# A bias tile that is loaded and masked half a unit ahead of its use, in a hybrid attention step

## The chip, the cores and the metric

One NeuronCore of a Trainium2 chip runs the whole step as one launch. The metric is the device time of a run in microseconds (us), from start to end of the program on the device; of several runs the median counts.

## The reference

One layer of a streaming encoder for 2048 prompt frames of width 1024 (and 32 sample frames, a small side job). `h = RMSNorm(x)`; one projection `z = h @ w_in` gives queries, keys, values and gates for two branches:

- A: chunk-band attention with 8 heads of 64. Frames come in chunks of 64; a frame sees its own chunk and the 8 before it, and its scores get a learned bias of the head, indexed by clipped distance: `scores = q·k / 8 + rel_bias[h, clip(i - j)]`, then softmax and `@ v`.
- B: differential attention, 4 heads with two q/k pairs of 64 and a value of 128. Two softmaxes over all earlier chunks, `p1 - lam * p2`, `@ v`, and an RMSNorm per head. No bias.

Both results are multiplied by `silu(gate)`, joined, projected by `w_out`, added to `x` and normed. New keys and values are outputs too.

## The kernel before, in words

**Units.** The work is cut into eight units, one for each weight slice of 512 columns: four A units (two heads each, u = 0 to 3) and four B units (one head each, u = 4 to 7). Line 701 sets the order: `[0, 4, 5, 1, 6, 2, 7, 3]`, so A, B, B, A, B, A, B, A. Each unit runs over 8 chunks of 256 frames (c = 0 to 7); `steps` (line 711) lists the 64 pairs (n, c) of unit number and chunk.

**A step** (loop of line 734). `chunk_qkv` projects the chunk (matmuls of lines 296 to 298 for keys and values, 303 to 305 for the transposed queries and the gate), every fp32 operand split in a high and a low part, and transposes keys and queries. `get_hT` loads the normed input of the next chunk (lines 261, 288, 289; two buffers). `attn_b` or `attn_a` computes scores (425, 426) and softmax. The second half of the attention (transposes 434, splits 438 and 439, the products with the values 450, and `finish_o` with lines 457 to 461, which stores the chunk's output with the DMA of line 461) is traced one step later, at the end of the step of the next chunk. So step c ends with the store of chunk c - 1.

**The bias.** In an A unit each score block goes through line 577 on VectorE (DVE), which adds a slice of the tile `bias` to the scores in PSUM, writes `ea` and takes the row maximum. `bias` is 128 x 2 x 640 in fp32 (640 KB, one buffer), loaded by one DMA of SyncE's queue (line 743, issued through the helper of line 146), and two corners of it are filled with -1e30 on GpSimd (POOL; lines 744 and 745), which masks what the band does not reach. Load and fills stand at c == 0 of the A unit, ahead of its `chunk_qkv`.

**What sets the order.** The program is traced in Python order, and a list scheduler puts each engine's instructions in one static order: by a priority (position in the trace, moved by `ahead(...)`) among what its own clock holds ready. At run time each engine works its list in order. `dma_here` (line 145) pins its DMA behind the DMA that was traced just before it on SyncE's queue. For the bias of unit n that is the store of line 461 of chunk 6 of unit n - 1, the last DMA traced in step (n - 1, 7). Three score tiles (`s_ps`), two transpose tiles (`t_ps`), one output tile (`o_ps`) and two projection tiles (`z_ps`) share PSUM.

The scheduler runs ahead across units: with the units at 345 to 570 us (n = 2, B) and then n = 3 (A), the projection of the A unit's chunk 0 is done while the B unit's last chunks are still in their attention.

Of the kernel before, what the change touches and what calls it, by code (L numbers as in the profile page):

```python
# [8 lines left out]
F32 = mybir.dt.float32  # L9
# [5 lines left out]
P = 128  # L15
# [9 lines left out]
NEG = -1.0e30  # L25
BAND = 640
# [4 lines left out]
def hybrid_step(  # L31
# [31 lines left out]
    PE, DVE, ACT, POOL, SP = nc.tensor, nc.vector, nc.scalar, nc.gpsimd, nc.sync  # L63
# [19 lines left out]
    pool = ctx.enter_context(tc.tile_pool(name="work", bufs=2))  # L83
# [61 lines left out]
    def dma_here(**kw):  # L145
        tc.keep_in_program_order(SP.dma_start(**kw))

    def small_loads():
        dma_here(out=ropec, in_=rope_c)
        dma_here(out=ropes, in_=rope_s)  # L150
        dma_here(out=gcol, in_=subln)
        DVE.tensor_scalar(gcol, gcol, 1.0 - LAMBDA_INIT, 0.0, ALU.mult, ALU.add)
        lt = e_tile("lt")
        lv = lt[:, 0:256].rearrange("p (a e) -> p a e", a=4)
        dma_here(out=lt[:, 0:256], in_=lams.broadcast_to([P, 256]))
        lp = lt[:, 256:384].rearrange("p (a e) -> p a e", a=2)
        DVE.tensor_tensor(lp, lv[:, 0:4:2, :], lv[:, 1:4:2, :], ALU.mult)
        ls = st_tile("ls", 2, 1)
        DVE.tensor_reduce(ls, lp, AX.X, ALU.add)
        le = st_tile("le", 2, 1)  # L160
        ACT.activation(le, ls, AF.Exp)
        DVE.scalar_tensor_tensor(nlam, le[:, 1:2], LAMBDA_INIT, le[:, 0:1], ALU.subtract, ALU.subtract)
        ACT.copy(out=lamc[NS:2 * NS], in_=nlam[NS:2 * NS])
# [6 lines left out]
    def load_w(wsrc, cur_b, gain=None, tags=(("w", 10),) * KT, raws=None):  # L170
        his, los = [], []
        for k in range(KT):
            raw = raw_w(wsrc, k, cur_b) if raws is None else raws[k]
            tag, bufs = tags[k]
            w = pool.tile([P, 2, 512], F32R, name="w", tag=tag, bufs=bufs)
            hi, lo = w[:, 0, :], w[:, 1, :]
            g = 1.0 if gain is None else gain[:, k:k + 1]
            if raws is not None:
                ACT.activation(hi, raw, AF.Copy, scale=g)  # L179
                DVE.scalar_tensor_tensor(lo, raw, g, hi.bitcast(F32), ALU.mult, ALU.subtract)  # L180
            elif cur_b and gain is not None and k % 2 == 0:
                ACT.activation(hi, raw, AF.Copy, scale=g)
                POOL.tensor_scalar(raw, raw, g, 0.0, ALU.mult, ALU.add)
                POOL.tensor_tensor(lo, raw, hi.bitcast(F32), ALU.subtract)
            else:
                POOL.tensor_scalar(hi, raw, g, 0.0, ALU.mult, ALU.add)
                DVE.scalar_tensor_tensor(lo, raw, g, hi.bitcast(F32), ALU.mult, ALU.subtract)
            his.append(hi)
            los.append(lo)
        return his, los  # L190
# [37 lines left out]
    def load_xT(c, js=range(4)):  # L228
        xs = [e_tile("xT").rearrange("p (k t) -> p k t", k=2) for _ in js]
        for x, j in zip(xs, js):  # L230
            SP.dma_start(out=x, in_=x_t[c, :, 2 * j:2 * j + 2, :])
        return xs

    def load_rows(c):
        return [load_x(x_pv[t * P:(t + 1) * P, :], P) for t in (2 * c, 2 * c + 1)]
# [40 lines left out]
    def make_hTs():  # L276
        h = norm_rows(load_x(x_sv, NS), NS)
        tp = t_psum()
        for k in range(KT):
            j = k % 4  # L280
            PE.transpose(out=tp[:, k * NS:(k + 1) * NS], in_=h[k // 4][0:NS, j * P:(j + 1) * P], identity=ident[0:NS, 0:NS])
        tv = tp[:, 0:KT * NS].rearrange("p (k t) -> p k t", k=KT)
        ACT.copy(out=hTs[:, :, 0:NS], in_=tv)
        DVE.tensor_tensor(hTs[:, :, NS:2 * NS], tv, hTs[:, :, 0:NS].bitcast(F32), ALU.subtract)
# [416 lines left out]
    order = [0, 4, 5, 1, 6, 2, 7, 3]  # L701
# [3 lines left out]
    def finish(gen, late):  # L705
        try:
            gen.send(late)
        except StopIteration:
            pass
# [10 lines left out]
    def get_hT(i):  # L720
        if i >= len(steps):
            return None
        n, c = steps[i]
        if n == 0:
            hT = make_hT(c, xts.pop(c))
            return hT
        return load_T(hT_d[c]), load_scales(c)
# [6 lines left out]
    for i, (n, c) in enumerate(steps):  # L734
        u = order[n]
        isB = u >= 4
        W = Ws[n]
        if c == 0:
            kss, vts = [], []
            bias = None  # L740
            if not isB:
                bias = pool.tile([P, 2, BAND], F32, name="bias", tag="bias", bufs=1)
                dma_here(out=bias, in_=bias_p[:, 2 * u:2 * u + 2, :])
                POOL.memset(bias[0:64, :, BAND - 64:BAND], NEG)
                POOL.memset(bias[64:128, :, 0:64], NEG)
        qkv = chunk_qkv(u, isB, c, hTn, W, kss, vts)
        QH, QL = next(qkv)
        gate = None
        if n == 0 and c + 2 < NCH:
            xts[c + 2] = load_xT(c + 2), load_rows(c + 2)  # L750
        hTn = get_hT(i + 1)
        if n == 0 and c == 1:
            small_loads()
        if n == 1 and c == 1:
            dma_here(out=aksv[0:PAST - NS, :], in_=cakv[NS:PAST, :])
            dma_here(out=avsv[0:PAST - NS, :], in_=cavv[NS:PAST, :])
        if n == 0 and c == NCH - 3:
            make_hTs()
        if c == NCH - 1 and n + 1 < len(order):
            v = order[n + 1]  # L760
            Ws[n + 1] = load_w(w_in[v // 4, v % 4], isB, ngain)
        prev = pend
        pend = attn_b(u, c, kss, vts, QH, QL) if isB else attn_a(u, c, kss, vts, QH, QL, bias)
        next(pend)
        late = (next(qkv), vts[c])
        if prev:
            finish(prev, plate)
        plate = late
        mid = n > 0 and not isB
        if c == 0 or (mid and c == 4):  # L770
            for _ in pend_s or ():
                pass
        if c == (2 if mid else NCH - 2):
            pend_s = sample_unit(u, isB, W)
            next(pend_s)
# [99 lines left out]
```

## Time and profile before

| | us |
|---|---|
| median of three runs (1591.02 to 1595.62) | 1593.42 |
| the profiled execution | 1592.68 |
| its span, first to last instruction | 1590.9 |
| TensorE matmul busy / weight load busy | 1537.6 / 1428.2 |
| DVE / ACT / POOL busy | 1097.6 / 1008.8 / 619.9 |

PE is TensorE's matmul row and PEld its weight loads, which overlap the matmuls; DVE is VectorE, ACT ScalarE, POOL GpSimd, SPq SyncE's queue, which issues every DMA here. The span is 1.8 us shorter than the time of the execution. A wait is read as `engine line <- what ended it`; it is idle time of the waiting engine just before that instruction. TensorE's granted clock is 0.990 of full speed over the span.

### The profile page before, as it was taken

What the parts mean: (1) busy time and instruction counts of PE and PEld (TensorE: products, weight loads), DVE (VectorE), ACT (ScalarE), POOL (GpSimd) and SP (SyncE); (2) the same over time, 40 slices, a digit from 0 to 9 for tenths busy, and PEclk for the clock granted to TensorE, in tenths of its full rate; (3) what the DMA queues carried; (4) which work ended last, traced back from release to release, by engine and by line L of the source; (5) the groups of instructions that cost most, each with busy time, mean ns of one, the idle gap of its engine ahead of it and who ended that gap; (6) DMA issues with size and microseconds to landing.
All of it is one profiled execution on the core that took longest, in us unless ns stands there. A gap on an engine that the chain in (4) does not pass through costs nothing.

```text
span 1590.9 us, 30369 instructions
## 1 busy us (share of the span) xinstructions
PE 1537.6 (97%) x10448; PEld 1428.2 (90%) x10448; DVE 1097.6 (69%) x3045; ACT 1008.8 (63%) x2706; POOL 619.9 (39%) x829
## 2 busy tenths in 40 slices
PE   7999999999999999999999999999999999999997
PEld 7999999888998889999998889999988899978885
DVE  5777768886689856577788756677888565853333
ACT  7885667776677766556777766657777665531111
POOL 5564424564346433343345522433445432520000
PEclk9999999999999999999999999999999999999999
DMA  9964454342442233536432233546432244635552
GB/s 368 366 250 156 166 190 140 112 148 85 174 157 92 71 115 111 196 133 231 143 139 80 91 142 127 186 146 230 148 111 101 90 142 151 235 131 181 167 208 69
DMA packets 105659, 249.65 MB, mean 157 GB/s; under 512 B 11192, under 2 KB 60480, under 8 KB 88064
## 3 DMA queue, kind: packets, MB, share of 16 engines
q1 hardware_dynamic: 105504, 247.70, 44.1%
q8 instruction: 83, 1.36, 0.3%
q14 instruction: 72, 0.59, 0.1%
HBM read 194.83 MB, written 53.75 MB: 156 GB/s over the span
## 4 chain that ended last, share of the span: by engine, by line
PE 80%; DVE 9%; ACT 3%; DMA 3%; issue 2%; POOL 2%; SPq 0%; DVEq 0%; ACTq 0%; POOLq 0%
PE z_ps L296 12%; PE z_ps L297 12%; PE z_ps L298 12%; PE o_ps L450 8%; PE t_ps L434 6%; PE s_ps L425 5%; PE z_ps L303 5%; PE s_ps L426 5%; PE z_ps L304 5%; PE z_ps L305 5%; DVE nmx L517 2%; DVE e L530 2%; DMA bias<-in_bias_p_dram 2%; DVE pl L439 1%; PE z_ps L310 1%
## 5 line engine op out<-in xcount | busy, mean ns | idle before, releaser
L296 PE MATMUL z_ps<-w,hT 128*128 128x256 f32 (+2 forms) x1280 | 421.5, 330 | 8.1 <-ACT w L179 6.5
L297 PE MATMUL z_ps<-w,hT 128*128 128x256 f32 (+2 forms) x1280 | 421.8, 330 | 2.0 <-DVE w L180 1.5
L298 PE MATMUL z_ps<-w,hT 128*128 128x256 f32 (+2 forms) x1280 | 420.8, 329 | 0.0
L296 PEld LDWEIGHTS z_ps<-w,hT 128*128 128x128 f32 x1280 | 243.0, 190 | 22.8 <-ACT w L179 6.5
L297 PEld LDWEIGHTS z_ps<-w,hT 128*128 128x128 f32 x1280 | 243.2, 190 | 17.8 <-DVE w L180 2.2
L298 PEld LDWEIGHTS z_ps<-w,hT 128*128 128x128 f32 x1280 | 243.2, 190 | 13.4
L519 ACT ACTIVATE e<-s_ps,nmx 128x512 f32<-128x512 f32 (+3 forms) x320 | 199.4, 624 | 87.5 <-DVE nmx L517 83.5
L439 DVE TENSOR_TENSOR pl<-t_ps,ph 128x512 fp32r<-128x512 f32 (+1 forms) x312 | 191.7, 623 | 66.8 <-ACT ph L438 63.1
L303 PE MATMUL z_ps<-hT,w 128*128 128x256 f32 x768 | 222.2, 289 | 5.6 <-DVE ql L391 5.6
L304 PE MATMUL z_ps<-hT,w 128*128 128x256 f32 x768 | 221.4, 288 | 0.0
L305 PE MATMUL z_ps<-hT,w 128*128 128x256 f32 x768 | 221.4, 288 | 0.0
L438 ACT CAST ph<-t_ps 128x512 fp32r<-128x512 f32 (+1 forms) x312 | 162.3, 535 | 70.6 <-PE t_ps L434 43.3
L425 PE MATMUL s_ps<-ks,qh 128*128 128x512 f32 (+2 forms) x544 | 194.1, 366 | 10.5 <-ACT e L519 8.6
L517 DVE TENSOR_REDUCE nmx<-s_ps 128x1 f32<-128x512 f32 (+3 forms) x320 | 188.8, 601 | 12.7 <-PE s_ps L426 9.4
L450 PE MATMUL o_ps<-ph,vt 128*128 128x256 f32 (+1 forms) x912 | 182.0, 274 | 8.1 <-DVE on L472 4.4
L426 PE MATMUL s_ps<-ks,ql 128*128 128x512 f32 (+2 forms) x544 | 188.1, 357 | 0.8 <-DVE ql L390 0.8
L525 POOL TENSOR_SCALAR e<-e,da 128x512 f32<-128x512 f32 (+3 forms) x160 | 112.6, 717 | 156.0 <-DVE da L495 103.4
L450 PE MATMUL o_ps<-pl,vt 128*128 128x256 f32 (+1 forms) x624 | 169.8, 311 | 0.1
L584 POOL TENSOR_SCALAR ea<-ea,sma 128x640 f32<-128x640 f32 (+4 forms) x128 | 96.8, 759 | 182.5 <-DVE sma L583 118.6
L450 PEld LDWEIGHTS o_ps<-ph,vt 128*128 128x128 f32 x912 | 149.4, 191 | 12.6 <-ACT ph L438 7.7
L303 PEld LDWEIGHTS z_ps<-hT,w 128*128 128x128 f32 x768 | 147.9, 193 | 9.7 <-DVE ql L391 6.7
L304 PEld LDWEIGHTS z_ps<-hT,w 128*128 128x128 f32 x768 | 147.8, 193 | 3.6 <-issue 1.3
(197 smaller groups left out, 3047.1 us busy)
## 6 DMA issues: line engine op xcount, KB each, us to landing
hT<-hTd SPq DMA_DIRECT2D x112, 1024.0 KB, 5.8
wraw<-in_w_in_dram SPq DMA_DIRECT2D x64, 256.0 KB, 4.9
hTd<-hT SPq DMA_DIRECT2D x8, 2048.0 KB, 9.4
oTd<-oT SPq DMA_DIRECT2D x64, 256.0 KB, 5.6
hT<-oTd SPq DMA_DIRECT2D x16, 1024.0 KB, 7.0
out_dram<-z SPq DMA_DIRECT2D x160, 64.0 KB, 1.6
xT<-in_x_t_dram SPq DMA_DIRECT2D x32, 256.0 KB, 5.2
xt<-in_x_prompt_dram SPq DMA_DIRECT2D x32, 256.0 KB, 5.7
```

The source lines that it names most:

```text
L296: PE.matmul(zp, hT[:, 0, k, ts], his[k][:, cols], start=(k == 0), stop=False)
L297: PE.matmul(zp, hT[:, 0, k, ts], los[k][:, cols], start=False, stop=False)
L298: PE.matmul(zp, hT[:, 1, k, ts], his[k][:, cols], start=False, stop=(k == KT - 1))
L303: PE.matmul(zp, his[k][:, cols], hT[:, 0, k, :], start=(k == 0), stop=False)
L304: PE.matmul(zp, his[k][:, cols], hT[:, 1, k, :], start=False, stop=False)
L305: PE.matmul(zp, los[k][:, cols], hT[:, 0, k, :], start=False, stop=(k == KT - 1))
L425: PE.matmul(sp[:, 0:w], QH[:, m, qs], ks[:, m, kc], start=True, stop=False)
L426: PE.matmul(sp[:, 0:w], QL[:, m, qs], ks[:, m, kc], start=False, stop=True)
L439: DVE.tensor_tensor(lv, tv, hv.bitcast(F32), ALU.subtract)
L450: PE.matmul(o, v, p, start=(first and n == 0), stop=(last and n == len(seq) - 1))
L517: DVE.tensor_reduce(nmx[:, m, b:b + 1], sp[:, 0:w], AX.X, ALU.max, negate=True)
L519: ACT.activation(e[:, 0:w], sp[:, 0:w], AF.Exp, bias=nmx[:, m, b:b + 1], accum_out=sm[:, m, b:b + 1])
```

## The change

The `bias` tile is now allocated, loaded and filled at c == 3 of the unit ahead of an A unit (in this order of units that is always a B unit: n = 2, 4 and 6). The first unit has none ahead of it and keeps its load at its own first step. Nothing else is changed: the same DMA, the same two fills, the same single buffer. By the trace order the DMA is now pinned behind the store of chunk 1 of that B unit.

```
         if c == 0:
             kss, vts = [], []
-            bias = None
-            if not isB:
-                bias = pool.tile([P, 2, BAND], F32, name="bias", tag="bias", bufs=1)
-                dma_here(out=bias, in_=bias_p[:, 2 * u:2 * u + 2, :])
-                POOL.memset(bias[0:64, :, BAND - 64:BAND], NEG)
-                POOL.memset(bias[64:128, :, 0:64], NEG)
+        nu = order[n + 1] if n + 1 < len(order) else 4
+        if (c == 3 and nu < 4) or i == 0:
+            lu = u if i == 0 else nu
+            bias = pool.tile([P, 2, BAND], F32, name="bias", tag="bias", bufs=1)
+            dma_here(out=bias, in_=bias_p[:, 2 * lu:2 * lu + 2, :])
+            POOL.memset(bias[0:64, :, BAND - 64:BAND], NEG)
+            POOL.memset(bias[64:128, :, 0:64], NEG)
         qkv = chunk_qkv(u, isB, c, hTn, W, kss, vts)
```

## Rows read from the trace of the kernel before

**Rows 1.** The page, part 1: busy time, share of the span and number of instructions of each engine.
```profile
PE 1537.6 (97%) x10448; PEld 1428.2 (90%) x10448; DVE 1097.6 (69%) x3045; ACT 1008.8 (63%) x2706; POOL 619.9 (39%) x829
```

**Rows 2.** The chain of waits that ended last, in order of time (start us, us, what): its longest pieces but for the first 15 us.
```profile
570.21 8.18 DMA bias<-in_bias_p_dram
...
911.30 8.72 DMA bias<-in_bias_p_dram
...
1252.75 8.12 DMA bias<-in_bias_p_dram
```

**Rows 3.** The tile `bias`: its instructions (ns min/median/max, first and last start in us), then the idle time before them and who waited for them (us in all, times).
```profile
L146 SPq DMA_DIRECT2D bias<-in_bias_p_dram x4: 639/947/968, 17.0 to 1252.8; - x4
L744 POOL MEMSET bias<- x4: 198/198/199, 27.3 to 1260.9; 64x128 f32 x4
...
  DMA bias<-in_bias_p_dram: 24.5, 4
...
  DVE ea L577: 7.6, 3
...
DMA to landing us min/median/max: 8.1/8.2/8.7
```

**Rows 4.** Timeline of SyncE's queue at the passage from unit n = 2 (B) to n = 3 (A): start us, us of issuing, line, DMA.
```profile
569.64 0.52 SPq L461 DMA_DIRECT2D oTd<-oT  x1
570.21 0.97 SPq L146 DMA_DIRECT2D bias<-in_bias_p_dram  x1
571.23 0.78 SPq L289 DMA_DIRECT2D hT<-hTd  x1
```

**Rows 5.** Timeline of the same passage, by engine: PE, POOL, DVE, ACT, PE (start us, us, engine, line, operation; in brackets the idle time before and what ended it). The first is the last matmul of three score blocks of A's chunk 0.
```profile
561.70 0.28 PE L426 MATMUL s_ps<-ks,ql 128*128 128x256 f32 x1
...
578.44 0.20 POOL L744 MEMSET bias<- 64x128 f32 x1 [6.47 <-DMA bias<-in_bias_p_dram]
...
578.68 0.29 DVE L577 CUSTOM_DVE_ANT_0 ea<-s_ps,bias 128x128 f32<-128x128 f32 x1 [2.39 <-POOL bias L744]
...
579.45 0.69 DVE L439 TENSOR_TENSOR pl<-t_ps,ph 128x512 fp32r<-128x512 f32 x1
...
580.23 0.40 ACT L582 ACTIVATE ea<-ea,nma 128x128 f32<-128x128 f32 x1 [3.51 <-DVE nma L580]
...
581.50 0.56 ACT L438 CAST ph<-t_ps 128x512 fp32r<-128x512 f32 x1
...
582.12 0.50 PE L450 MATMUL o_ps<-ph,vt 128*128 128x256 f32 x2 [0.62 <-ACT ph L438]
```

**Rows 6.** Timeline of DVE at the same point of the other two passages (n = 4 to 5, n = 6 to 7).
```profile
920.30 0.29 DVE L577 CUSTOM_DVE_ANT_0 ea<-s_ps,bias 128x128 f32<-128x128 f32 x1 [2.93 <-POOL bias L744]
...
1261.16 0.29 DVE L577 CUSTOM_DVE_ANT_0 ea<-s_ps,bias 128x128 f32<-128x128 f32 x1 [2.33 <-POOL bias L744]
```

**Rows 7.** Busy time by stretch (stretch, its us, busy us and instructions of PE, PEld, DVE, ACT and POOL, granted clock, DMA share, GB/s): 12 us from 1.3 us behind the first L577 of each of the three passages; then 12 us just behind the passage from B to B (n = 1 to 2), which has no bias, 12 us in the middle of an A unit, and at last three slices of 4 us ahead of the first L577 of n = 3.
```profile
580.00:592.00 12.00, 11.15 (x83) 9.74 (x82) 6.03 (x24) 8.98 (x28) 3.44 (x8) 1.00 0.05 14
921.60:933.60 12.00, 11.05 (x83) 9.68 (x81) 6.01 (x24) 8.98 (x28) 3.43 (x8) 1.00 0.05 14
1262.50:1274.50 12.00, 11.21 (x84) 9.81 (x82) 6.01 (x24) 8.98 (x28) 3.43 (x8) 1.00 0.05 14
...
376.00:388.00 12.00, 11.57 (x84) 11.43 (x85) 7.25 (x20) 7.40 (x20) 4.46 (x7) 1.00 0.15 46
600.00:612.00 12.00, 12.00 (x100) 11.79 (x99) 8.69 (x34) 8.54 (x25) 4.75 (x9) 1.00 0.18 60
...
568.00:572.00 4.00, 4.00 (x37) 4.00 (x36) 1.88 (x4) 3.13 (x7) 1.54 (x3) 1.00 0.43 69
572.00:576.00 4.00, 4.00 (x36) 4.00 (x36) 0.76 (x2) 1.06 (x2) 0.00 (x0) 1.00 1.00 373
576.00:580.00 4.00, 4.00 (x36) 4.00 (x35) 1.61 (x8) 0.59 (x1) 0.40 (x2) 1.00 0.83 345
```

**Rows 8.** The same view, the whole of the passage from B to B (36 us), then of the three passages from B to A, 40 us each.
```profile
364.00:400.00 36.00, 33.56 (x224) 30.70 (x223) 21.89 (x60) 20.74 (x55) 12.80 (x18) 0.95 0.29 97
560.00:600.00 40.00, 36.84 (x274) 32.76 (x273) 20.20 (x58) 23.15 (x62) 14.27 (x22) 1.00 0.41 144
901.00:941.00 40.00, 35.84 (x263) 31.56 (x262) 19.55 (x57) 23.53 (x63) 14.27 (x22) 1.00 0.40 137
1242.50:1282.50 40.00, 36.17 (x269) 32.09 (x268) 20.16 (x58) 23.54 (x63) 14.26 (x22) 1.00 0.41 143
```

**Rows 9.** Timeline of SyncE's queue around the store of chunk 1 of the units n = 2, 4 and 6.
```profile
438.51 0.52 SPq L461 DMA_DIRECT2D oTd<-oT  x1
440.68 4.47 SPq L362 DMA_DIRECT2D out_dram<-z  x2
...
782.00 0.33 SPq L288 DMA_DIRECT2D hT<-hTd  x1
782.41 0.52 SPq L461 DMA_DIRECT2D oTd<-oT  x1
782.99 0.74 SPq L289 DMA_DIRECT2D hT<-hTd  x1
...
800.68 0.33 SPq L288 DMA_DIRECT2D hT<-hTd  x1
...
1123.85 0.52 SPq L461 DMA_DIRECT2D oTd<-oT  x1
```

**Rows 10.** Timeline of POOL in the same places, n = 2 and n = 4.
```profile
449.22 1.25 POOL L525 TENSOR_SCALAR e<-e,da 128x512 f32<-128x512 f32 x2 [3.02 <-DVE s_ps L516]
...
785.49 1.26 POOL L525 TENSOR_SCALAR e<-e,da 128x512 f32<-128x512 f32 x2 [3.63 <-PE o_ps L450]
...
793.80 1.36 POOL L525 TENSOR_SCALAR e<-e,da 128x512 f32<-128x512 f32 x2 [4.38 <-DVE da L495]
```

**Rows 11.** Busy time by stretch (columns of Rows 7) around the store of chunk 1 of the units n = 2, 4 and 6.
```profile
432.00:460.00 28.00, 28.00 (x176) 26.47 (x175) 22.29 (x61) 21.18 (x58) 12.66 (x16) 1.00 0.50 179
776.00:808.00 32.00, 32.00 (x213) 30.58 (x213) 26.34 (x71) 24.51 (x69) 14.42 (x21) 1.00 0.46 161
1116.00:1148.00 32.00, 32.00 (x212) 30.49 (x211) 25.86 (x70) 23.14 (x66) 14.36 (x20) 1.00 0.43 145
```

**Rows 12.** DMA issues of the stretch 780 to 792 us (KB each, median us from issue to landing).
```profile
hT<-hTd SPq DMA_DIRECT2D x2, 1024.0 KB, 5.7
```

## The prediction, made before the result was known

> **What bounds the kernel now.** I read the engines' totals first. TensorE's matmul row is busy for 1537.6 of 1590.9 us, its weight loads for 1428.2, and no other engine is above 1097.6 [rows 1]. So a change pays only where TensorE stands still or runs thin. Next I read the chain of waits that ended last: among its longest pieces are three transfers of the bias, 8.18, 8.72 and 8.12 us, at 570, 911 and 1253 us, the three passages from a B unit to an A unit [rows 2]. That is 25.0 us of chain, but not 25.0 us to win, since the chain shows one way back and TensorE has other work meanwhile. Third, the tile's own view: POOL stands 24.5 us before the fills over four loads, and DVE 7.6 us behind them over three [rows 3].
>
> Then one passage in detail. SyncE issues the bias load at 570.21, right behind the store at line 461 that it is pinned to [rows 4]. Three score blocks of A's chunk 0 have been in PSUM since about 562, and line 577 can take the first only at 578.68, when POOL has waited 6.47 us for the data and filled the corners [rows 5]. DVE works its list in order: behind line 577 stand its part of the B unit's last value products (line 439, 579.45) and, on ACT behind the exponentials, line 438 at 581.50; TensorE, which got by with projections until then, waits 0.62 us for it at 582.12 [rows 5]. DVE's waits at the three passages are 2.39, 2.93 and 2.33 us, 7.65 in all [rows 5, 6].
>
> What TensorE loses behind the load is in the windows. In the 12 us from 1.3 us after the first line 577, matmuls are busy for 11.15, 11.05 and 11.21 us and weight loads for 9.74, 9.68 and 9.81; in the middle of an A unit it is 12.00 and 11.79 [rows 7].
>
> **The change, part by part.** The kernel still makes four loads and eight fills; three loads and six fills move. The first unit keeps its load and its wait, 24.5 less 19.9 (6.47, 7.02 and 6.42), some 4.6 us on POOL [rows 3]: no change there.
>
> *Gain at the passages.* The load leaves 570.21 and goes to the store of chunk 1, at 438.51, 782.41 and 1123.85 [rows 9], over 125 us ahead of the first line 577. With 8.1 to 8.7 us to landing [rows 3] it is long there, so POOL's and DVE's waits at the passages vanish in any case. What that is worth to TensorE I bound from three rows. Low end: only time in which no matmul runs comes back, 0.85 + 0.95 + 0.79 = 2.6 us [rows 7]. Middle: weight loads come back to the pace of the middle of an A unit, (11.79 - 9.74) + (11.79 - 9.68) + (11.79 - 9.81) = 6.1 us; against the passage from B to B, which has no bias (11.43), it is 5.1 [rows 7]. High end for a plain shift: DVE's whole stall, 7.65 us. I take 6.1: it lies nearest to the stall that is removed, and the rows behind it show line 439 and line 438, on which TensorE's products hang, coming late by that stall and not by the matmul gaps alone.
>
> A rule of the Trainium skill bears on this choice (Perfetto Trace Analysis, "Identifying the Most-Contended Engine"): matmul busy time is a poor measure of TensorE's headroom, and weight-load busy time is to be used. By matmul busy time the sum would be 2.6 us, by weight loads 6.1; no run here shows yet which holds.
>
> What is late next at the passage: TensorE's own shares of the B unit's last products and the chunk-1 projection, then the single `o_ps` tile that B's last chunk, the sample job and A's chunk 0 use in turn. That is why I don't count the whole 11.2 us of TensorE's matmul gaps in the three 40 us passages (3.16 + 4.16 + 3.83) [rows 8].
>
> *SyncE's queue.* At the old place the 0.97 us of issuing and the 640 KB leave the gap between the two halves of an `hT` load [rows 4]; that tile is not needed for many microseconds, so I price it at nothing. At the new place the same 0.97 us lands in front of the second half of an `hT` load (782.99) or of key and value stores (440.68) [rows 9]. An `hT` load lands 5.7 us after issue [rows 12], and the next one goes out at 800.68, when the buffer in use is given up [rows 9]; so the tile issued at 782 has some 18 us before its first use, and a delay of an issue (0.97) and at most the bias's own 8.7 us is covered. Without that cover it would cost 3 x 0.97 to 3 x 8.7 us. I take nothing.
>
> *POOL's queue.* The fills cost 2 x 0.2 us each time at either place. New is that POOL must wait for the load in the middle of a B unit if the scheduler lists the fills ahead of the landing. Queued behind them would be the gate product (line 337), the value split (404) and the scaling of the exponentials (525), for which DVE and then TensorE's transposes wait. At n = 2 a load issued at 439.0 lands at about 447.3, ahead of line 525 at 449.22: it costs nothing on the path [rows 9, 10]. At n = 4 (and n = 6, alike) it is issued at about 782.9 and lands at 791.1, while line 525 stands at 785.49: a wait of up to 5.6 us, twice 11.2 [rows 3, 9, 10]. The bounds are 0 and 11.2 us. I take 0: in these stretches TensorE's matmuls are busy for 28.00 of 28.00 and 32.00 of 32.00 us and POOL for less than half [rows 11], while POOL stands 3.0 to 4.4 us at a time there already [rows 10], so TensorE has work queued that covers such a wait.
>
> *The schedule.* A's first softmax may be listed sooner, and with it the score tiles be freed sooner, 16 us at most [rows 5]; orders behind it may shift either way. I bound that by the gaps of the passages, +11.2 to -11.2 us, and take nothing.
>
> **Sum.** Against the profiled execution: 1592.68 - 6.1 = 1586.6 us. The median of the runs shown is 0.74 us above that execution, so 1593.42 - 6.1 = 1587.3 us for the median.
>
> **Rivals.** No change (within 0.3%, or 4.8 us, about what a measurement of this kernel can tell from no change; the three runs lie 4.6 us apart): the passage is bound by TensorE's own work, and only the matmul gaps come back: 1593.4 - 2.6 = 1590.8 us. For it: matmuls run without a gap from 568 to 580 while the load is awaited, and the passage from B to B, with no bias, loses time as well (33.56 of 36 us busy) [rows 7, 8]. Against it: behind that passage weight loads are at 11.43 of 12 us, not 9.7 [rows 7].
>
> Slower: the wait moves to POOL in the B unit. The fills stand right behind their load in the trace, so the scheduler may list them ahead of line 525 by a landing that comes too soon on its clock; then POOL's 5.6 us delay at n = 4 and 6 reaches the transposes. It decides as soon as the landing is later than line 525's release and TensorE's queued work runs out within 5.6 us: 1593.4 - 2.6 + 11.2 is 1602.0 with the small gain, 1598.5 with mine; I take 1598.5. For it: at the passages POOL did stand 6.4 to 7.0 us at just these fills [rows 3, 5]. Against it: POOL's present waits of 3.0 to 4.4 us leave TensorE full [rows 10, 11].
>
> The Trainium skill has a rule for this (DMA: Bandwidth & Descriptors, "Rules for kernel authors"): issue a load early and wait on its semaphore late. The change does the first; for the fills on POOL it waits early, and by that half of the rule the result would be the slower one, 1598.5; the rows show the cover but no fill there yet.
>
> Faster still: with the bias there, A's chunk 0 is spread into TensorE's holes at 560 to 568 and all matmul gaps of the passages go, 11.2 us [rows 8]: 1582.3. Against it: much of these gaps belongs to B's last softmax, and the passage from B to B has 2.4 us of them without a bias [rows 8].
>
> That the change doesn't do what it says is hardly possible: the buffer was last read in the A unit before the B unit, which is over by then, and the pin is to a store that is out long before.
>
> **How the numbers follow.** My forecast (a gain of 4.8 to 9 us) gets 0.45, faster still 0.09, no change 0.33, slower 0.13. So faster by over 0.3% (under 1588.6) is 0.54, same 0.33, slower 0.13. The range runs from 1580, which holds the case of 1582.3 and leaves perhaps 0.05 below, to 1598.5, the slower case as priced, with perhaps 0.06 above it. The forecast's own range is 1584.4 to 1588.6.
>
> **What would show it.** Right: three loads at about 439, 783 and 1124 us; no wait of DVE for line 744 at the passages; weight loads near 11.4 us in the 12 us behind the first line 577 there; no bias transfer in the chain but the first. Wrong: POOL waiting over 4 us before line 744 in the B units with gaps of TensorE at lines 434 or 450 just after; or weight loads still at 9.7 in the passages, with another releaser of DVE and ACT; or the gain given back in chunk 4 to 7 of the B units.

## The result, and the profile after

The changed kernel takes 1584.57 us in the median of four runs (1583.67 to 1586.67), the kernel before beside it 1593.66 (1591.02 to 1595.62): a ratio of 0.9946, 95% interval 0.9928 to 0.9964. It was timed twice more on other occasions: 1589.23 us against 1593.48 (0.9967, 0.9955 to 0.9979) and 1587.32 against 1594.00 (0.9958, 0.9946 to 0.9970). Over its 15 runs the median is 1586.89 us. By the three comparisons the change is worth some 4 to 9 us; the first one showed the upper end. The profiled execution took 1585.08 us, with a span of 1583.3 at a granted clock of 0.993; before it was 1592.68, 1590.9 and 0.990.

The page's totals after, the line of [rows 1]:

```profile
PE 1535.1 (97%) x10448; PEld 1425.9 (90%) x10448; DVE 1095.4 (69%) x3045; ACT 1006.4 (64%) x2706; POOL 622.4 (39%) x829
```

The work is the same; what went is time in which TensorE stood or ran thin. The tile `bias`, as in [rows 3] (the lines behind 739 stand one lower in the changed kernel, so the fills are L745 and L746):

```profile
L146 SPq DMA_DIRECT2D bias<-in_bias_p_dram x4: 599/600/1100, 18.2 to 1118.9; - x4
L745 POOL MEMSET bias<- x4: 197/198/198, 28.0 to 1123.6; 64x128 f32 x4
...
  DMA bias<-in_bias_p_dram: 10.5, 3
...
  POOL bias L745: 10.5, 3
```

POOL's wait for the load fell from 24.5 us to 10.5, and nobody waits for POOL's fills any more: the 7.6 us of `DVE ea L577` are gone. No bias transfer stands in the chain that ended last, where there were 25 us of them [rows 2]. The loads on SyncE's queue now stand right behind the store of chunk 1, where [rows 9] showed the place:

```profile
438.46 0.60 SPq L146 DMA_DIRECT2D bias<-in_bias_p_dram  x1
...
784.29 0.60 SPq L146 DMA_DIRECT2D bias<-in_bias_p_dram  x1
...
1118.90 0.60 SPq L146 DMA_DIRECT2D bias<-in_bias_p_dram  x1
```

POOL's first fill in the three B units, to be held against [rows 10] (in brackets the idle time before it and what ended it):

```profile
443.95 0.20 POOL L745 MEMSET bias<- 64x128 f32 x1 [1.26 <-DMA bias<-in_bias_p_dram]
...
790.22 0.20 POOL L745 MEMSET bias<- 64x128 f32 x1 [1.96 <-ACT ks L383]
...
1123.63 0.20 POOL L745 MEMSET bias<- 64x128 f32 x1 [4.63 <-DMA bias<-in_bias_p_dram]
```

At n = 6 POOL stands 4.63 us for the landing, as the slower rival had it, and it reaches nobody: matmuls are busy for 32.00 of the 32 us from 1111 there.

At the passages, busy time by stretch (columns of [rows 7]): first 12 us at the places of [rows 7], then the 40 us of [rows 8], both moved by what the kernel is ahead.

```profile
580.00:592.00 12.00, 12.00 (x95) 10.97 (x94) 4.88 (x13) 7.33 (x20) 1.79 (x4) 1.00 0.04 12
916.50:928.50 12.00, 12.00 (x98) 11.22 (x97) 5.25 (x11) 6.59 (x17) 0.57 (x2) 1.00 0.05 13
1255.00:1267.00 12.00, 12.00 (x96) 11.17 (x95) 4.54 (x12) 6.79 (x20) 2.53 (x5) 1.00 0.04 13
...
560.00:600.00 40.00, 37.80 (x273) 34.24 (x272) 19.50 (x58) 23.33 (x63) 13.89 (x20) 0.96 0.36 125
896.00:936.00 40.00, 39.27 (x299) 35.64 (x298) 20.48 (x60) 23.57 (x64) 13.99 (x22) 1.00 0.34 120
1235.00:1275.00 40.00, 38.17 (x280) 33.67 (x279) 20.03 (x59) 24.89 (x69) 13.79 (x20) 1.00 0.35 125
```

The thin 12 us behind the load are full of matmuls again. But the 40 us rows show that the three passages did not gain alike: the second does 299 matmul records where it did 263, the first 273 where it did 274, and the first alone has a granted clock of 0.96.

**Where the time went, stretch by stretch.** TensorE does the same matmuls in both kernels. I counted its work up by the columns of each matmul and took the difference of the times at which both kernels have done as much (minus: ahead of the kernel before). The table gives how that difference changes from one time of the kernel before to the next, in us, for the profiled execution of every kernel in this text; dummy matmuls are not counted. The first passage is the stretch from 557 to 583 us, the second from 891 to 941, the third from 1225 to 1274. Each line is one execution: that of `only_n2` was the fastest of its eleven, that of `at_c5` the slowest of its eleven. `after_again` and `after_third` are the changed kernel of the later two comparisons; the other names are told below.

```
             to     first   583 to A to B  758 to second  941 to 1177 to third   to
             557    passage 737    737-758 891    891-941 1177   1225    1225-74 end    all
after        -0.2   +0.0    -0.2   +2.9    -2.2   -5.5    +1.2   -1.9    -1.3    -0.5   -7.6
after_again  +1.7   +0.0    -0.2   +2.2    -2.3   -5.5    +1.2   -0.2    +0.0    -0.5   -3.4
after_third  -0.9   +0.0    -0.2   +1.8    -0.0   -5.5    +1.2   -1.9    -1.3    -0.5   -7.3
fill_after   +1.0   -1.5    -0.2   +4.3    -2.1   -5.5    +1.2   -1.7    -1.3    -0.5   -6.2
fix_p1       -1.0   -1.5    -0.2   +4.5    -2.2   -5.5    +1.2   -0.8    +0.2    -0.3   -5.5
old_lists    -0.3   -1.3    +0.6   -0.0    -0.0   +0.6    -0.0   +0.1    -1.3    -0.1   -1.9
old_again    +1.8   -1.3    +0.1   +0.0    -1.1   -0.3    +0.0   -0.2    +0.2    +0.8   -0.1
fill_old     +1.4   -1.3    +0.3   -0.0    -0.1   -1.9    +0.0   -0.1    -1.3    -0.3   -3.3
late_fills   +0.8   -1.4    -0.2   +4.4    -0.3   -2.2    +0.5   -1.2    -1.5    -0.3   -1.3
only_n2      -1.2   -1.4    -0.2   +1.7    +1.0   -2.8    +1.0   +1.3    -1.7    -0.4   -2.7
only_n4      -0.9   +0.6    -0.2   +0.0    +0.7   -1.2    +1.1   -1.6    +1.6    -0.6   -0.3
at_c5        +0.6   +0.0    -0.2   +1.9    +0.1   -0.5    +0.5   +0.1    +1.1    -0.4   +3.2
shift3       +3.1   +0.5    +0.7   +0.0    +0.7   +0.8    +0.8   -0.4    +2.1    -0.3   +7.8
```

For the changed kernel (first line): nothing at the first passage, 5.5 us at the second, 1.3 at the third, 4.1 in the late chunks of the B units n = 4 and 6, where the change touches nothing, and 2.9 us lost at the passage from A to B (n = 3 to 4), where it touches nothing either. A total of 7.6 near the forecast's 6.1, then, by terms that the forecast did not have. The experiments ask why.

### The profile page after: what moved, and what is told of

The parts are those of the page before. It is cut to its first block, busy times and chain, and to the rows that moved or that the text cites. A ratio compares the mean times of both kernels' runs of the same rounds, so it can differ in the third digit from the quotient of the medians.

```text
span 1583.3 us, 30355 instructions
## 1 busy us (share of the span) xinstructions
PE 1535.1 (97%) x10448; PEld 1425.9 (90%) x10448; DVE 1095.4 (69%) x3045; ACT 1006.4 (64%) x2706; POOL 622.4 (39%) x829
## 4 chain that ended last, share of the span: by engine, by line
PE 75%; DVE 10%; ACT 4%; POOL 4%; issue 4%; DMA 3%; SPq 0%; DVEq 0%; POOLq 0%; ACTq 0%
PE z_ps L296 11%; PE z_ps L297 11%; PE z_ps L298 11%; PE o_ps L450 8%; PE t_ps L434 6%; PE s_ps L425 5%; PE z_ps L304 4%; PE z_ps L303 4%; PE s_ps L426 4%; PE z_ps L305 4%; DVE nmx L517 2%; POOL e L525 1%; DVE e L530 1%; DVE pl L439 1%; DMA xt<-in_x_prompt_dram 1%
## 5 line engine op out<-in xcount | busy, mean ns | idle before, releaser
L439 DVE TENSOR_TENSOR pl<-t_ps,ph 128x512 fp32r<-128x512 f32 (+1 forms) x312 | 192.5, 623 | 60.1 <-ACT ph L438 56.2
```

The lines of the kernel that those rows point to most:

```text
L439: DVE.tensor_tensor(lv, tv, hv.bitcast(F32), ALU.subtract)
```

## The experiments

Theory 1: each passage gives back its own wait, about 2 us by the forecast's 6.1, about 3 by the 9.1 first measured. Theory 2: the wait is worth little, and the time comes from the order of the lists, which the scheduler makes anew when the bias is traced elsewhere. In the course a third came up, from the granted clock: in the traces it is 0.50 of full speed (1.2 GHz instead of 2.4) in short stretches, and these lie in other places from list to list, and in part from one execution to the next. In all comparisons the kernel before stands at 1593.4 to 1594.0 us.

**One load alone.** Only the bias of unit n = 3 (`only_n2`), or of unit n = 5 (`only_n4`), is traced early, by `soon = (2,)` or `(4,)` (the edit against the changed kernel):

```
-        if (c == 3 and nu < 4) or i == 0:
-            lu = u if i == 0 else nu
+        soon = (2,)
+        if (c == 3 and nu < 4 and n in soon) or (c == 0 and not isB and n - 1 not in soon):
+            lu = nu if isB else u
```

> Only the bias of unit 3 is loaded and filled early (at chunk 3 of unit 2); units 5 and 7 keep their load at their own chunk 0. If each passage gains by its own wait (theory 1), this gains a third of the 9.1 us, about 3 us against the kernel before. If the gain comes from the new order of lists and not from the wait (theory 2), nothing is gained here, since TensorE's progress in the trace of after is level with before through this passage (-0.1 us at 583, +0.1 at 606) and then 2.9 us worse at 740 to 757: 0 to +3 us.

> Only the bias of unit 5 is loaded and filled early (at chunk 3 of unit 4). Theory 1: about 3 us faster than before. Theory 2: most of the gain stands here, 5 to 8 us, as TensorE's progress in the trace of after gains 7.6 us between 842 and 941 us.

Measured: 1592.66 us, ratio 0.9994 (0.9986 to 1.0003), and 1595.33, ratio 1.0011 (1.0001 to 1.0020). The wait at the passage in question went both times (POOL's waits 19.8 and 14.6 us in place of 24.5), yet neither kernel is faster, and one is a little slower. In the table the edited passage does gain, 1.4 us at n = 2 and 1.2 at n = 4; elsewhere the lines of the table differ by 1 to 3 us in stretches that the edit doesn't touch. `only_n2` even gains 2.8 us at the second passage and 1.7 at the third, where POOL still waits 6.17 and 7.55 us for the load. So the sum of single gains is not the gain, against theory 1. Theory 2 missed as well: it expected 5 to 8 us from `only_n4`.

**Another place for the load, and for the fills.** `at_c5` traces load and fills at chunk 5 (`soon = (2, 4, 6)`, `c == 5`). `late_fills` traces the load at chunk 3 and the fills where the kernel before did (the edit against the changed kernel):

```
             dma_here(out=bias, in_=bias_p[:, 2 * lu:2 * lu + 2, :])
+        if c == 0 and not isB:
             POOL.memset(bias[0:64, :, BAND - 64:BAND], NEG)
             POOL.memset(bias[64:128, :, 0:64], NEG)
```

> All three loads and fills at chunk 5 of the B unit in place of chunk 3; the bias is there long before its use in either. Theory 1: the same time as the changed kernel, 1584.6 within 2 us. Theory 2: a time of its own, more than 3 us away from it on either side.

> The load at chunk 3 of the B unit as in the change, the two fills left at chunk 0 of the A unit as before. Theory 1: the load's wait is what counted, the fills are 0.4 us: the same as the changed kernel, 1584.6 within 2 us, and no wait of POOL in the B units. Theory 2: another time, more than 3 us away.

Measured: 1595.04 us, ratio 1.0003 (0.9994 to 1.0012), and 1591.96, ratio 0.9989 (0.9981 to 0.9998). Both lie over 7 us from the changed kernel's first 1584.57, as theory 2 had it, and 2.7 us or more from its highest median, 1589.23. Neither has a wait of DVE for a fill. But `late_fills` doesn't fill late: the scheduler listed the fills ahead, and they ran in the B units, at 445.64, 791.79 and 1133.17 us. So it differs from the changed kernel in the lists and not in the place of the work. POOL of `late_fills` at n = 4:

```profile
791.79 0.20 POOL L746 MEMSET bias<- 64x128 f32 x1 [6.56 <-DMA bias<-in_bias_p_dram]
```

`late_fills` gains at all three passages (1.4, 2.2 and 1.5) and pays 4.4 back at the passage from A to B. `at_c5` gains next to nothing at the passages (0.0, -0.5 and +1.1) and loses 1.9 from A to B. All the waits at the passages are gone in both, and the times lie 3 us apart. Part of that goes with the clock: in the 8 us from 564, 905 and 1248 us `at_c5` has 0.79, 0.79 and 0.60, `late_fills` 1.00 in all three. The second of these, `at_c5` and then `late_fills` (columns of [rows 7]; the clock is the third from the end):

```profile
905.00:913.00 8.00, 5.96 (x34) 5.35 (x32) 5.26 (x24) 5.71 (x17) 7.13 (x9) 0.79 0.00 0
```

```profile
905.00:913.00 8.00, 5.35 (x42) 4.85 (x41) 7.08 (x25) 6.33 (x18) 7.51 (x10) 1.00 0.00 0
```

So what is listed where, with the clock that comes with it, weighs as much as the wait.

**The lists held fixed.** To take the scheduler out, the program is built twice: the first build gives the static list of each engine, the list is edited, and the second build holds every engine to it. In `old_lists` all lists are those of before, and only the three loads are moved, on SyncE's list:

```
    ...
    for lu, ahead_u in ((1, 5), (2, 6), (3, 7)):
        sp.remove(("bias", lu, 0))
        sp.insert(sp.index(("store", ahead_u, 1)) + 1, ("bias", lu, 0))
```

`shift3` is the counterpart: no load moves, but `tc.cur_priority` is raised by 3 at chunk 3 of units 2, 4 and 6 and lowered by 3 behind the bias of the next unit, as the three traced instructions do in the changed kernel.

> Every engine follows the static list of the kernel before, instruction by instruction (the list is taken from a first build and imposed by issue-order edges); only the three loads of the bias move on SyncE's list, to the place behind the store of chunk 1 where the change has them. The fills keep their old place. So the wait goes and no order changes. The plain shift of the prediction: DVE's 7.65 us of stalls go, 6.1 us faster than before. If the wait is hidden by TensorE's other work: 0 to 2.6 us faster.

> The kernel before with its late load; only the scheduler's priority counter is raised by 3 at chunk 3 of units 2, 4 and 6 and lowered by 3 behind the bias of the unit after it, as the three moved instructions do. No work, load or wait changes, only the lists that come out. If the order of the lists is a large term by itself, this is off from before by 2 us or more on either side; if the lists matter little, it is within 1 us of before.

Measured: 1593.04 us, ratio 0.9987 (0.9977 to 0.9997); a second time (`old_again`) 1590.89, ratio 0.9984 (0.9975 to 0.9992). `shift3` 1597.58, ratio 1.0030 (1.0018 to 1.0042). So new lists alone, with the clock that comes with them, can cost 4 us with no load moved. The loads alone gain 2.1 to 2.6 us by ratio: not the 6.1 us of the plain shift, but within the 0 to 2.6 us expected if TensorE's other work hides the wait. The rest of the changed kernel's 4 to 9 us came with its new lists, the earlier place of the fills among them. But in the table `old_lists` gains 1.3 us at the first and at the third passage and loses 0.6 at the second, where the same wait was removed. The busy time and clock of that place, first the kernel before, then `old_lists` (columns of [rows 7]):

```profile
904.00:912.00 8.00, 6.19 (x51) 5.95 (x52) 4.60 (x10) 5.04 (x13) 5.71 (x6) 1.00 0.13 20
```

```profile
904.00:912.00 8.00, 6.42 (x33) 6.42 (x34) 4.04 (x8) 3.30 (x8) 4.59 (x5) 0.57 0.09 16
```

33 matmuls in place of 51, in about the same busy time (6.42 and 6.19 us), so slow ones: a mean clock of 0.57 over 8 us is 6.9 us at 0.50 (8 x 0.43 / 0.5). TensorE's waits just ahead of it, from the timeline of `old_lists`:

```profile
903.04 0.88 PE L434 MATMUL t_ps<-ident,e 128*128 128x128 f32 x6 [1.39 <-DVE e L530]
905.58 0.58 PE L303 MATMUL z_ps<-hT,w 128*128 128x256 f32 x1 [1.66 <-DVE ql L391]
```

Before has the same two waits 1.1 us later and keeps its clock at 1.00:

```profile
904.15 0.87 PE L434 MATMUL t_ps<-ident,e 128*128 128x128 f32 x6 [1.37 <-DVE e L530]
906.69 0.39 PE L303 MATMUL z_ps<-hT,w 128*128 128x256 f32 x1 [1.66 <-DVE ql L391]
```

So the same pair of gaps does or doesn't cost the clock, and one cannot read from the list which. Within the 22 executions of `old_lists` and `old_again`, the nine with a mean clock up to 0.988 have a median of 1593.27 us, the four with 0.992 or more 1587.70.

**The changed kernel, its first passage.** There the late piece is no wait for the bias. POOL and DVE of the changed kernel, from their timelines:

```profile
567.04 1.63 POOL L584 TENSOR_SCALAR ea<-ea,sma 128x128 f32<-128x128 f32 x4
568.63 0.74 POOL L457 TENSOR_TENSOR og<-on,gate 128x256 f32<-128x256 f32 x1
```

```profile
561.40 0.28 DVE L577 CUSTOM_DVE_ANT_0 ea<-s_ps,bias 128x128 f32<-128x128 f32 x1
...
569.40 0.42 DVE L331 TENSOR_TENSOR gate<-z_ps,rb 128x256 f32<-128x256 f32 x1 [1.53 <-POOL og L457]
```

DVE serves A's first score block at 561.40, 17 us sooner than at 578.68 [rows 5]. A's scalings (line 584) are therefore ready sooner, are listed ahead of B's store work (line 457) and hold up DVE's gate by 1.53 us (0.85 before). At the second passage the same freedom seems to fall out well, which no run tested by itself: there POOL has line 457 ahead of the long scalings of line 525 (kernel after, then before):

```profile
901.69 0.74 POOL L457 TENSOR_TENSOR og<-on,gate 128x256 f32<-128x256 f32 x1 [0.34 <-DVE dr L493]
...
903.00 3.13 POOL L525 TENSOR_SCALAR e<-e,da 128x512 f32<-128x512 f32 x4
```

```profile
902.20 3.13 POOL L525 TENSOR_SCALAR e<-e,da 128x512 f32<-128x512 f32 x4 [5.81 <-DVE da L495]
...
908.42 0.74 POOL L457 TENSOR_TENSOR og<-on,gate 128x256 f32<-128x256 f32 x1 [0.18 <-DVE on L472]
```

`fix_p1` keeps the lists of the changed kernel and moves the four scalings of the first passage behind that store work:

```
    ...
    four = [k for k in pl if k[:3] == ("scale", 1, 0)]
    for k in four:
        pl.remove(k)
    at = pl.index(("ol", 5, 6)) + 1
    pl[at:at] = four
```

> The changed kernel itself, beside the others on one chip: 1584.6 us, 9 us faster than before, as measured; the yardstick for the next one.

> The changed kernel's own lists, imposed, with one edit: at the first passage POOL's four scalings of A's chunk 0 (1.6 us) go behind the gate product and the store work of B's chunk 6, as they were listed before. If these four are what gave the passage's gain back (the gate product started at 568.63 in place of 567.34 us), this is 1.3 us faster than the changed kernel; if not, the same within 0.5 us.

Measured: `fix_p1` 1585.53 us (1584.09 to 1587.17), ratio 0.9950 (0.9938 to 0.9962), against 1589.23 (1586.05 to 1590.80) for the changed kernel in the same comparison, 3.7 us less where 1.3 were expected; the intervals of the two ratios overlap a little. It is the faster of the two there; the changed kernel's first four runs were as fast. At the first passage it gains the 1.5 us that the changed kernel lacks. That it also kept the clock at 1.00 there (0.79 in the changed kernel) left two causes: the order on POOL, or the clock.

**The clock by itself.** Dummy transposes of the identity go into one of TensorE's gaps, with every list as it was. `fill_old` is `old_lists` with eight of them where TensorE waits for line 530 in the last chunk of each B unit ahead of an A unit, written into the transpose tile that is open; `fill_after` is the changed kernel with eight in the one gap of the first passage in which TensorE waits for line 391, written into the score tile that the sample job uses next.

```
-            PE.transpose(out=tp[:, i * P:(i + 1) * P], in_=b, identity=ident)
+            tr = PE.transpose(out=tp[:, i * P:(i + 1) * P], in_=b, identity=ident)
+            if mark:
...
+                if fill and mark[0] > 4 and (mark[1], i) == (0, 0) and FILL_AT == "t":
+                    for k in range(N_FILL):
+                        tags["fill", mark[0], k] = PE.transpose(out=tp[:, P:2 * P], in_=ident, identity=ident)
```

> The kernel with the lists of before and only the three loads moved on SyncE's queue, once more, so that the kernel with dummy work in one gap has its twin on the same chip. Both theories: about 1593 us (1593.04 the first time). The theory of the clock: its profile shows a stretch at half clock behind the passage at 904 us, as the first one did, or its time is near 1587 where it shows none. The theory of the lists: its time does not go with the clock of the run.

> As the one before it, with eight dummy transposes of the identity (some 1 us of TensorE) in the gap of 1.4 us in which TensorE waits for DVE's line 530 in the last chunk of each B unit ahead of an A unit; they are written into a transpose tile that is held already and are overwritten by the transposes that wait. The theory of the clock (the wait that went is worth about 6 us, and TensorE's stretches at half clock behind gaps take some of it): no stretch at half clock at 904, which was 6.8 us long, up to 3.4 us back, so about 1590 us. The theory of the lists (what is listed where sets the time, the clock only goes along): dummy work in a gap gives nothing, 1593 us, or up to 3 us more where it delays what waits.

> The changed kernel once more, as the twin of the next one on the same chip. Both theories: between its two medians so far, 1584.6 and 1589.2 us. The theory of the clock: a stretch at half clock behind the first passage (566 to 568 us), and a time that falls as the granted clock of the run rises.

> The changed kernel with its own lists, and eight dummy transposes (some 1 us) in one gap alone: the 1.6 us in which TensorE waits for DVE's line 391 at the first passage (564 to 565.6 us). The theory of the clock: no stretch at half clock at 566 to 568, which was 3.4 us long, so up to 1.7 us less than the twin, and at the end of the first passage TensorE is about 1.3 us ahead of where it was without them, as it was when POOL's scalings were moved there. The theory of the lists: no difference from the twin (within 0.5 us), since the scalings of A still stand ahead of the store work of B on POOL.

Measured: `fill_old` 1590.53 us over eleven executions (ratio 0.9975, 0.9966 to 0.9985; a twelfth of 3010.7 us is left out of both), its twin `old_again` 1590.89; `fill_after` 1587.14 (0.9957, 0.9945 to 0.9969), its twin `after_third` 1587.32. At the place itself the answer is plain. `fill_old`, timeline of TensorE and the same 8 us (its L439 is the dummy; lines behind 434 stand up to five lower):

```profile
902.88 1.04 PE L439 MATMUL t_ps<-ident 128*128 128x128 f32 x8
904.42 0.87 PE L434 MATMUL t_ps<-ident,e 128*128 128x128 f32 x6 [0.50 <-DVE e L535]
906.95 0.39 PE L303 MATMUL z_ps<-hT,w 128*128 128x256 f32 x1 [1.66 <-DVE ql L391]
```

```profile
904.00:912.00 8.00, 5.92 (x49) 5.69 (x50) 4.82 (x9) 5.03 (x12) 5.96 (x6) 1.00 0.05 14
```

The first gap is 0.50 us instead of 1.39, the clock stays at 1.00, and the second passage gains 1.9 us where `old_lists` lost 0.6 and `old_again` (0.79 in these 8 us) gained 0.3. The first passage of the changed kernel, `after_third` and then `fill_after`:

```profile
564.00:572.00 8.00, 7.22 (x48) 7.22 (x49) 3.66 (x11) 4.06 (x13) 5.30 (x8) 0.79 0.21 48
```

```profile
566.00:574.00 8.00, 7.31 (x61) 7.31 (x62) 4.88 (x13) 5.10 (x15) 5.25 (x8) 1.00 0.38 124
```

```profile
564.89 1.04 PE L663 MATMUL s_ps<-ident 128*128 128x128 f32 x8
566.69 0.39 PE L303 MATMUL z_ps<-hT,w 128*128 128x256 f32 x1 [0.77 <-DVE ql L391]
```

61 matmuls in place of 48, and a gain of 1.5 us where all three profiles of the changed kernel, each with a clock of 0.79 there, gained nothing. POOL's order is untouched in `fill_after`, and DVE waits there for line 457 (its L462) as long as before:

```profile
570.53 0.42 DVE L331 TENSOR_TENSOR gate<-z_ps,rb 128x256 f32<-128x256 f32 x1 [1.53 <-POOL og L462]
```

So in these profiles (one of `fill_after`, three of the changed kernel) it was the clock, not line 457 behind line 584, that took the first passage's gain. The theory of the lists is refuted for this place.

The medians moved for neither pair, though, as the theory of the lists had expected, against the 3 us and 1.7 us that the theory of the clock allowed. The table shows why for these profiles: `fill_after` lost 4.3 us at the passage from A to B, `after_third` 1.8, and they differ by 1.9 us before 557 us, where the lists are the same; `fill_old` and `old_again` stand 1.4 and 1.8 us behind before by then. Keeping the clock in one place does not keep it in the others, which differ between executions of one program, and five rounds of runs that lie 3 to 7 us apart don't resolve 1.5 us.

**Not settled.** The loss at the passage from A to B. Part of it goes with the clock here too: the three kernels that lose 4.3 to 4.5 us (`fill_after`, `fix_p1`, `late_fills`) have a clock of 0.79 in the 8 us from 738, the five that lose 1.7 to 2.9 (the changed kernel three times, `only_n2`, `at_c5`) have 1.00. First `fix_p1`, then the changed kernel:

```profile
738.00:746.00 8.00, 7.09 (x38) 6.68 (x37) 4.23 (x9) 4.09 (x10) 2.01 (x3) 0.79 0.53 184
```

```profile
738.00:746.00 8.00, 5.76 (x37) 4.93 (x36) 5.64 (x10) 4.60 (x13) 4.13 (x5) 1.00 0.84 304
```

The other 1.7 to 2.9 us stay open. POOL there waits longer for a weight tile, though its load is issued at about the same time, and the next pair is issued later; SyncE's queue, then POOL of the changed kernel, and POOL of before:

```profile
732.03 1.34 SPq L167 DMA_DIRECT2D wraw<-in_w_in_dram  x2
...
739.95 1.48 SPq L167 DMA_DIRECT2D wraw<-in_w_in_dram  x2
```

```profile
738.02 0.69 POOL L186 TENSOR_SCALAR w<-wraw,ngain 128x512 fp32r<-128x512 f32 x1 [5.39 <-DMA wraw<-in_w_in_dram]
```

```profile
735.53 0.69 POOL L186 TENSOR_SCALAR w<-wraw,ngain 128x512 fp32r<-128x512 f32 x1 [1.71 <-DMA wraw<-in_w_in_dram]
```

Kernels with the lists of before don't lose there, those listed anew with the first of the three loads early lose 1.7 to 4.5 us. Which instruction of the lists does it was not tried. Nor could the counterpart of `old_lists` be, the lists of the changed kernel with the load at its old place: they put A's softmax ahead of where that load would land.

## Why the prediction was right, and where it was not

The time was forecast as 1587.3 us and came out as 1584.57, 1589.23 and 1587.32; the sign and the range held, and two of the three lie in the forecast's own 1584.4 to 1588.6, the third just outside. That the size held is luck in good part. The loads alone, with the lists of before, gained 2.1 to 2.6 us in the whole time (4.0 by ratio in `fill_old`); 2.6 us is the price of the rival "no change". The rest came with the new lists, which the forecast took as nothing. Step by step:

*The path.* Right. The loads leave at 438.46, 784.29 and 1118.90 (forecast about 439, 783, 1124), DVE doesn't wait for a fill at any passage, the chain has no bias transfer, and weight loads in the 12 us come to 10.97, 11.22 and 11.17 us (forecast near 11.4).

*The gain at the passages, 6.1 us.* Right in kind and too large. Counted at the passages alone, with no stretch at half clock in them, `fill_old` gives 1.3 + 1.9 + 1.3 = 4.5 us and `late_fills`, with lists of its own, 1.4 + 2.2 + 1.5 = 5.1: between the low end by matmul gaps (2.6) and the 6.1 by weight loads. I let the weight loads come back to 11.79 of 12 us, the middle of an A unit; in the changed kernel they come back to 11.0 to 11.2, a rise of 33.36 - 29.23 = 4.1 us over the three windows, while matmul gaps give 36.00 - 33.41 = 2.6. The passage from B to B (11.43), which the prediction had beside it, gives 5.1. The Trainium skill says not to judge TensorE's headroom by matmul busy time but, among other things, by weight-load busy time (Perfetto Trace Analysis, "Identifying the Most-Contended Engine"). The gain at the passages agrees in so far as weight loads lie nearer to it; by the whole time of `old_lists` the matmul gaps lie nearer, so the runs don't decide it. How far the weight loads come back also depends on where the window is put, as the first passage of `old_lists` shows:

```profile
578.00:590.00 12.00, 12.00 (x97) 11.17 (x95) 5.35 (x19) 8.64 (x26) 3.51 (x8) 1.00 0.05 16
580.00:592.00 12.00, 12.00 (x90) 10.31 (x89) 5.29 (x15) 8.59 (x27) 3.34 (x7) 1.00 0.09 25
```

*SyncE's queue at nothing.* Right: 0.60 us of issuing in each place, no later wait for `hT` in the chain.

*POOL's queue at nothing.* Right, and the wait that the slower rival feared was there: 4.63 us at n = 6 with TensorE at 32.00 of 32.00 (the 1.2 us lost between 941 and 1177 are lost before 1100, ahead of this load). The Trainium skill's rule to issue a load early and wait on its semaphore late (DMA: Bandwidth & Descriptors, "Rules for kernel authors") names no price for a wait that comes early; in this trace it cost TensorE nothing, since POOL, the engine that waited, had slack.

*The schedule, taken as nothing.* This is the step that failed, within its bound of 11.2 us. The lists gave 3.6 us at the second passage (5.5 against 1.9 with the old lists), where the matmul gaps of the 40 us fell from 4.16 to 0.73, as the faster rival had it for all three; which instruction of the lists did it was not tried. They took 1.8 to 2.9 us at the passage from A to B. Half-clock stretches took the first passage's 1.5 us, and two of before's (clock 0.79 in the 8 us from 852 and from 1194) are not in the changed kernel's first profile, which is 2.2 and 1.9 us better there:

```profile
852.00:860.00 8.00, 7.07 (x39) 6.64 (x40) 6.59 (x17) 4.79 (x15) 6.83 (x8) 0.79 0.43 165
...
1194.00:1202.00 8.00, 7.64 (x44) 7.21 (x45) 6.59 (x17) 5.13 (x16) 6.27 (x7) 0.79 0.36 140
```

```profile
852.00:860.00 8.00, 7.38 (x56) 6.78 (x55) 7.92 (x21) 7.04 (x22) 7.20 (x8) 1.00 0.82 320
...
1188.00:1196.00 8.00, 7.47 (x57) 6.83 (x56) 7.17 (x17) 6.03 (x18) 6.46 (x7) 1.00 0.88 298
```

With the same lists the gain of 2.2 us is 0.0 in `after_third`, whose clock is 0.79 in the 8 us from 862, so this gain goes with the clock. That these terms add up to something near the forecast is luck of this list: `at_c5` loses its waits too and is no faster than before. The chance of 0.33 for no change was therefore not too high.

## What to carry to other kernels

Price a removed wait by what TensorE's weight loads regain over the stretch behind it, measured against a neighbouring passage; here that came to 5.1 us, against 4.5 to 5.1 found at the passages, but only 2.1 to 2.6 in the whole time of `old_lists`. Where a list scheduler orders the work, then, add some 5 us either way on this kernel for the new lists, and to tell the edit from the lists, impose the old lists on the edited program and compare TensorE's progress stretch by stretch. Look at the granted clock of a stretch before explaining a difference of a few microseconds in it.

## What the runs showed of the hardware

TensorE's granted clock fell to 0.50 (1.2 GHz) behind gaps far shorter than a transfer: behind 1.39 and 1.66 us of standing with 0.9 us of work between them, for 6.9 us in one kernel (33 matmuls in 8 us instead of 51) and not at all in another with nearly the same two gaps (1.37 and 1.66 us). Such a stretch cost 1.5 us where the clock was 0.79 over 8 us (`after_third` against `fill_after`) and 2.5 us where it was 0.57 (`old_lists` against `fill_old`). Eight dummy transposes, 1.04 us of work in a gap, kept the clock at that place in the two profiles taken, while the medians of the whole time did not move beyond the noise.
